# Modulation rows of a two-layer diffusion backbone: 128x2048 float32 pieces in four 32-column strips of the TensorE array, in place of 128x1024 pieces in 512-column blocks

## The chip, the cores and the metric

The kernel runs on one core of one Trainium2 chip. A core has five engines with instruction streams of their own: TensorE (PE, matrix products; its weight loads are shown apart as PEld), VectorE (DVE), ScalarE (ACT), GpSimd (POOL) and SyncE (SP, which only issues transfers here). They share an on-chip memory of 128 partitions (SBUF) and the accumulators that TensorE writes (PSUM); transfers to and from DRAM are moved by 16 DMA engines. Each engine works through its own instructions in order and waits on semaphores of the others.

The metric is the device time of one execution in microseconds (us). Before the change it is 3449.05 us, the median of three runs (3446.75 to 3449.51).

## The reference

Two layers work on 1024 latent tokens and 256 context tokens of width 1024. Layer 0 has neighbourhood attention beside a bidirectional mLSTM, layer 1 a bidirectional gated linear recurrence (HGRN2). What matters here is the modulation: each layer turns a conditioning vector into a shift, a scale and a gate of 1024 numbers each, once for the latent tokens (from `c`) and once for the context (from `c_ctx`).

```python
def _ada(cvec, w, b):
    m = jax.nn.silu(cvec) @ w + b
    return jnp.split(m.reshape((-1, 1, m.shape[-1])), 3, axis=-1)

for l in range(DEPTH):                       # DEPTH = 2, w_ada: (2, 1024, 3072) float32
    shift, scale, gate = _ada(c, w_ada[l], b_ada[l])
    shift_c, scale_c, gate_c = _ada(c_ctx, w_ada[l], b_ada[l])
    h_lat = _rms(x, norm_w[l]) * (1.0 + scale) + shift
    h_ctx = _rms(ctx, norm_w[l]) * (1.0 + scale_c) + shift_c
    ...                                      # the layer's mixer gives y_lat, y_ctx
    x = x + gate * y_lat
```

So two rows (`c` and `c_ctx`) are multiplied by a 1024x3072 matrix in each layer: 25 MB of weights in all for two rows of result. Columns 0 to 2047 of a layer are shift and scale, columns 2048 to 3071 the gate.

## The kernel before

**Precision and the main products.** Large products take each float32 operand as a sum of two parts in the faster type float32r, a high and a low one (`split`: a copy on ACT makes the high part, a subtraction on DVE the low part), and add three products (`dense`, lines 128 to 130: high by high, low by high or high by low). Their PSUM tiles are named `mm`.

**The first stage (the page's first 85 us).** The scope `pre` computes the modulation of layer 0 (`ada(0, pool, False)`), then normalizes ten tiles of 128 tokens (`x`; squares on ACT into `njk`, the inverse root `nr` on POOL, the scaling on DVE), transposes them on PE (line 238), applies scale and shift (`ntmp`) and splits the result into `hh` and `hl`, the input of every later projection. Meanwhile `na_values(0)` makes the first block of attention values on PE as far as `hh` and `hl` are there.

For layer 0, `ada_rows` loads the weights in pieces of 128x2x512 float32 (512 KB; two k-slices of 128 rows, 512 columns) through SP's queue. Each k-slice is one plain float32 product (line 179): the two conditioning rows stand in the array (128x2) and 512 columns of weights stream past. 4 blocks of 512 columns by 8 k-slices are 32 such products. A plain float32 product leaves two records in the trace, so they are 64 records. Each block ends with a copy on ACT (`adarow`, line 182) and four small products with the 2x2 identity `sel` (line 194) that turn the row into columns.

**The second stage (85 to about 250 us).** The scope `gates` computes the gates of the mLSTM (`ml_gates`), the gate rows of layer 0 (`ada_gate(0)`), shift and scale of layer 1 (`ada(1, pool, True)`), the gate rows of layer 1 (`ada_gate(1)`), and then `na_values(1)`, ten tiles of 128 tokens by 512 value columns (`proj_wide`). Here the modulation goes through the split: every piece of 512 KB comes through POOL's queue into one of three buffers (`adar`), ACT makes `adah` (128x1024), DVE makes `adal`, and PE does two float32r products for each k-slice and block (line 176 with four stationary columns, line 177 with two), 128 in all. A gate block ends with one product with `sel` (line 214) and a transfer to DRAM (`gated`), which is read only at the ends of the two layers.

**What sets the order.** A scheduler goes through the program in the order of the code, with a model of the chip, and puts each engine's instructions in a fixed order; `filler()` lowers the priority of the work in it, so that it is put where an engine would otherwise wait. What it has put in order, an engine does in that order. Tiles come from pools: a tile of a scope that opens can be written only when the tiles of the closed scope that lay in the same place are no longer read.

Of the kernel before, what the change touches and what calls it, by code (L numbers as in the profile page):

```python
# [44 lines left out]
class Prog:  # L45
# [114 lines left out]
    def ada_rows(self, l, blk, pool, parts):  # L160
        nc = self.nc
        wv = self.a["wada"][l].rearrange("(k p) f -> p k f", p=P)
        ps = self.ps("ad", [4, 512])
        for k in range(0, KD, 2):
            raw = self.t(pool, [P, 2, 512], F32, "adar", self.adab)
            self.last_dma = (nc.gpsimd if parts else nc.sync).dma_start(
                out=raw, in_=wv[:, k : k + 2, blk * 512 : (blk + 1) * 512]
            )
            if parts:
                hi = self.t(pool, [P, 2, 512], F32R, "adah", 2)  # L170
                lo = self.t(pool, [P, 2, 512], F32R, "adal", 2)
                self.split(hi, lo, raw)
            for j in range(2):
                first, last = k + j == 0, k + j == KD - 1
                if parts:
                    nc.tensor.matmul(ps, lhsT=self.sc4[:, k + j, :], rhs=hi[:, j, :], start=first, stop=False)
                    nc.tensor.matmul(ps[0:2], lhsT=self.sc4[:, k + j, 0:2], rhs=lo[:, j, :], start=False, stop=last)
                else:
                    nc.tensor.matmul(ps[0:2], lhsT=self.sc[:, k + j, :], rhs=raw[:, j, :], start=first, stop=last)
        rows = self.t(pool, [4, 512], F32, "adarow", 2)  # L180
        n = 4 if parts else 2
        nc.scalar.copy(rows[0:n], ps[0:n])
        return rows[0:n]

    def ada(self, l, pool, parts):
        nc, a = self.nc, self.a
        ab = self.ab[l]
        pss = self.t(pool, [P, 16, 2], F32, "adass", 1)
        for blk in range(4):
            rows = self.ada_rows(l, blk, pool, parts)  # L190
            p4 = self.ps("tr", [P, 4, 2])
            n = rows.shape[0]
            for m in range(4):
                nc.tensor.matmul(p4[:, m, :], lhsT=rows[:, m * P : (m + 1) * P], rhs=self.sel[0:n], start=True, stop=True)
            nc.vector.tensor_copy(pss[:, blk * 4 : blk * 4 + 4, :], p4)
        for v in range(2):

            nc.vector.tensor_tensor(out=ab[:, 1, v, :], in0=pss[:, 0:8, v], in1=self.badap[:, l, 0:8], op=ALU.add)
            nc.vector.tensor_tensor(out=ab[:, 0, v, :], in0=pss[:, 8:16, v], in1=self.badap[:, l, 8:16], op=ALU.add)
            nc.vector.scalar_tensor_tensor(  # L200
                out=ab[:, 0, v, :], in0=ab[:, 0, v, :], scalar=1.0, in1=self.normw[:, l, :], op0=ALU.add, op1=ALU.mult
            )

    def ada_gate(self, l, pool):
        nc, a = self.nc, self.a
        for blk in range(4, 6):
            s = slice((blk - 4) * 512, (blk - 3) * 512)
            gr = self.t(pool, [2, 512], F32, "grow", 1)
            bg = self.t(pool, [2, 512], F32, "bgrow", 1)
            for v in range(2):  # L210
                nc.sync.dma_start(out=bg[v : v + 1, :], in_=a["bada_g"][l : l + 1, s])
            rows = self.ada_rows(l, blk, pool, True)
            psg = self.ps("tr", [2, 512])
            nc.tensor.matmul(psg, lhsT=self.sel, rhs=rows, start=True, stop=True)
            nc.vector.tensor_tensor(out=gr, in0=psg, in1=bg, op=ALU.add)
            nc.sync.dma_start(out=self.gated[l, :, s], in_=gr)
# [50 lines left out]
    def na_values(self, b, pool=None):  # L267
        c0 = b * 256
        if pool:
            self.proj_wide(2 * D + c0, lambda s: self.vd[s, c0 : c0 + 512], pool, range(NT))  # L270
        else:
            self.proj_out(2 * D + c0, self.vd[:, c0 : c0 + 256])


    def proj_wide(self, c0, dst, pool, order, gate=None):
# [3 lines left out]
        for tt in order:  # L279
# [10 lines left out]
            nc.gpsimd.dma_start(out=d, in_=v)  # L290

# [71 lines left out]
    def ml_gates(self, pool, keep):  # L363
# [782 lines left out]
    def build(self):  # L1146
        tc, nc, a = self.tc, self.nc, self.a
        dma = nc.sync.dma_start
        with ExitStack() as es:
# [43 lines left out]
            self.sc4 = self.t(cp, [P, KD, 4], F32R, "sc4")  # L1193
            self.split(self.sc4[:, :, 0:2], self.sc4[:, :, 2:4], self.sc)
            self.sel = load("sel", [4, 2])
# [25 lines left out]
            with self.pp.phase(ad=2), tc.tile_pool(name="pre", bufs=2) as pool:  # L1221
# [390 lines left out]
```

## Time and profile before

| what | us |
|---|---|
| median of three runs | 3449.05 |
| the profiled execution | 3449.74 |
| its span, first to last instruction | 3448.0 |
| PE busy in the span | 3388.6 (98%) |
| DVE busy | 2089.0 (61%) |
| ACT busy | 1443.8 (42%) |
| POOL busy | 669.7 (19%) |

The profile is that of one execution. A row of a timeline reads: start, time until the last of the merged instructions ends, engine, line, operation, tiles written and read, shapes, count; in brackets how long the engine had been idle and what ended that. A matmul's duration includes its way through the array, so matmuls overlap in the records; how fast they follow one another is read from start to start. In a table of windows each engine's busy time stands beside the granted clock of TensorE (1.00 is full) and what the DMA engines moved.

### The profile page before, as it was taken

Reading aid. Unit: us, or ns where it says so; the run is one execution under the profiler, and the core shown is the slowest. Engines: PE = TensorE matmul, PEld = TensorE weight load, DVE = VectorE, ACT = ScalarE, POOL = GpSimd, SP = SyncE. Lnnn points to the kernel's source line nnn. Section 1 sums busy time; section 2 is a strip of 40 time slices with the busy share of each in tenths; the row PEclk is TensorE's granted clock in tenths of the full one; section 3 lists DMA queues with packets and bytes.
Section 4 is the critical chain, followed back from the end, with each engine's and each line's share of the span. In section 5 each row is a group of like instructions: output and inputs, shape, how many; then the busy total and the mean of one; then the engine's idle time right before and its main releaser. Section 6 shows DMA issues by size and latency. Waiting matters only on the chain.

```text
span 3448.0 us, 64658 instructions
## 1 busy us (share of the span) xinstructions
PE 3388.6 (98%) x25100; PEld 2988.2 (87%) x25100; DVE 2089.0 (61%) x4824; ACT 1443.8 (42%) x3353; POOL 669.7 (19%) x1044
## 2 busy tenths in 40 slices
PE   8999999999999999999999999999999999999987
PEld 5679998899989888898888999999999999989876
DVE  4536666666655556687656555555555555565667
ACT  5445544554443434454444333333333333333432
POOL 2222221222221112221100111111111111131023
PEclk9999999999999999999999999999999999999999
DMA  5542222322223434444653111111111111121374
GB/s 207 175 130 61 80 75 81 90 81 69 76 87 100 147 104 127 137 136 143 209 167 96 47 56 59 59 56 59 59 59 56 56 48 47 46 71 38 114 213 147
DMA packets 331539, 333.59 MB, mean 97 GB/s; under 512 B 30984, under 2 KB 277960, under 8 KB 331232
## 3 DMA queue, kind: packets, MB, share of 16 engines
q1 hardware_dynamic: 291008, 222.76, 21.9%
q0 software_dynamic: 40224, 106.69, 9.1%
q8 instruction: 198, 3.24, 0.4%
q14 instruction: 109, 0.89, 0.1%
HBM read 259.40 MB, written 69.79 MB: 95 GB/s over the span
## 4 chain that ended last, share of the span: by engine, by line
PE 91%; DVE 3%; DMA 2%; issue 1%; ACT 1%; POOL 0%; SPq 0%; POOLq 0%; DVEq 0%; ACTq 0%
PE mm L130 20%; PE mm L128 20%; PE mm L129 20%; PE s L1006 4%; PE acc L783 3%; PE tr L763 2%; PE mm L843 2%; PE mm L845 2%; PE mm L844 2%; PE acc L555 2%; PE s L564 2%; PE acc L545 1%; PE acc L1082 1%; PE acc L1083 1%; PE acc L1084 1%
## 5 line engine op out<-in xcount | busy, mean ns | idle before, releaser
L128 PE MATMUL mm<-hh,wh 128*128 128x512 f32 (+1 forms) x1600 | 582.2, 364 | 0.0
L130 PE MATMUL mm<-hh,wl 128*128 128x512 f32 (+1 forms) x1600 | 582.0, 364 | 0.0
L129 PE MATMUL mm<-hl,wh 128*128 128x512 f32 (+1 forms) x1600 | 581.7, 364 | 0.0
L128 PE MATMUL mm<-wh,hh 128*128 128x256 f32 (+1 forms) x1520 | 472.6, 311 | 1.3 <-ACT ev L317 0.6
L129 PE MATMUL mm<-wl,hh 128*128 128x256 f32 (+1 forms) x1520 | 471.6, 310 | 0.0
L130 PE MATMUL mm<-wh,hl 128*128 128x256 f32 (+1 forms) x1520 | 470.9, 310 | 0.0
L130 PEld LDWEIGHTS mm<-hh,wl 128*128 128x128 f32 x1600 | 301.9, 189 | 44.8 <-issue 0.2
L128 PEld LDWEIGHTS mm<-hh,wh 128*128 128x128 f32 x1600 | 302.1, 189 | 42.9 <-issue 0.5
L129 PEld LDWEIGHTS mm<-hl,wh 128*128 128x128 f32 x1600 | 302.0, 189 | 41.8 <-issue 0.2
L128 PEld LDWEIGHTS mm<-wh,hh 128*128 128x128 f32 x1520 | 290.0, 191 | 15.5 <-issue 1.1
L129 PEld LDWEIGHTS mm<-wl,hh 128*128 128x128 f32 x1520 | 289.9, 191 | 14.3 <-issue 2.9
L130 PEld LDWEIGHTS mm<-wh,hl 128*128 128x128 f32 x1520 | 289.9, 191 | 12.8 <-issue 1.7
L128 PE MATMUL mm<-wzh,hh 128*128 128x256 f32 x1024 | 293.8, 287 | 0.0
L130 PE MATMUL mm<-wzh,hl 128*128 128x256 f32 x1024 | 289.1, 282 | 0.0
L129 PE MATMUL mm<-wzl,hh 128*128 128x256 f32 x1024 | 288.6, 282 | 0.0
L73 DVE TENSOR_TENSOR wl<-wraw,wh 128x512 fp32r<-128x512 f32 x240 | 168.5, 708 | 119.4 <-ACT wh L72 113.0
L72 ACT CAST wh<-wraw 128x512 fp32r<-128x512 f32 x240 | 147.2, 619 | 211.9 <-PE mm L129 156.1
L128 PEld LDWEIGHTS mm<-wzh,hh 128*128 128x128 f32 x1024 | 192.9, 188 | 2.2
L129 PEld LDWEIGHTS mm<-wzl,hh 128*128 128x128 f32 x1024 | 192.8, 188 | 1.8
L130 PEld LDWEIGHTS mm<-wzh,hl 128*128 128x128 f32 x1024 | 192.7, 188 | 1.2
L843 PE MATMUL mm<-woh,yh 128*128 128x512 f32 x422 | 171.9, 407 | 14.8 <-ACT yh L72 8.3
L1036 ACT COPY gksel<-gK 128x1024 f32<-128x1024 f32 x96 | 111.0, 1156 | 178.1 <-PE s L1006 123.4
(391 smaller groups left out, 7518.2 us busy)
## 6 DMA issues: line engine op xcount, KB each, us to landing
wraw<-in_wab_dram SPq DMA_DIRECT2D x112, 256.0 KB
wraw<-in_wc_dram SPq DMA_DIRECT2D x96, 256.0 KB
wraw<-yd SPq DMA_DIRECT2D x94, 256.0 KB
adar<-in_wada_dram POOLq DMA_DIRECT2D x32, 512.0 KB, 4.4
wraw<-in_wc_dram SPq DMA_DIRECT2D x128, 128.0 KB
md<-ev POOLq DMA_DIRECT2D x60, 256.0 KB, 2.8
mloz<-md SPq DMA_DIRECT2D x40, 256.0 KB
adar<-in_wada_dram SPq DMA_DIRECT2D x16, 512.0 KB
```

Source lines behind the costliest of these rows:

```text
L72: nc.scalar.copy(hi, x)
L73: nc.vector.tensor_tensor(out=lo, in0=x, in1=hi.bitcast(F32), op=ALU.subtract)
L128: mm(ps, lhsT=lh(k), rhs=rh(k), start=(start and k == 0), stop=False)
L129: mm(ps, lhsT=lh(k), rhs=rl(k), start=False, stop=False)
L130: m = mm(ps, lhsT=ll(k), rhs=rh(k), start=False, stop=(stop and k == nk - 1))
L555: nc.tensor.matmul(num, lhsT=qc[:, j, :], rhs=C[d][:, j, :], start=False, stop=(j == 1))
L564: nc.tensor.matmul(u, lhsT=st["k"][c][:, j * P : (j + 1) * P], rhs=vw, start=True, stop=True)
L763: nc.tensor.transpose(pt[:nk, i, :], pr[:, o : o + nk], self.ident)
L783: m = nc.tensor.matmul(yp[h64], lhsT=v[:, h64], rhs=pTs[hd][:nk, i, :], start=(i == turn[0]), stop=(i == turn[-1]), tile_position=(0, hd * ...
L843: mm(ps, lhsT=yh[k], rhs=w.h(kk), start=(kk == 0), stop=False)
L1006: self.nc.tensor.matmul(out[s], lhsT=lhsT, rhs=rhs, start=True, stop=True, tile_position=(0, b * 64))
L1036: nc.scalar.copy(ksel.rearrange("p (b s i) -> p b s i", s=2, i=h), pick(K))
```

## The change

The change makes the modulation everywhere from the raw float32 weights, without the split.

- A piece of weights is now 128 rows by 2048 columns (1 MB). `ada_rows` returns eight steps for one output; a step loads a piece (`chunk`) and issues four plain float32 products, one for each 512 columns. The two conditioning rows are the first two of 32 stationary columns (`sc32`, the rest is zero, set in `wide_c`), and product j takes the strip of 32 columns of the array, and of 32 partitions of one PSUM tile, that begins at 32j (`tile_position`).
- Shift and scale of a layer are one output (2048 columns). The gates of both layers are another (1024 columns from each layer, so two transfers of 512 KB for a piece). There are 8 steps for layer 0, 8 for layer 1 and 8 for the gates, 32 products for each eight.
- An output of shift and scale ends with one copy on ACT (128x512), four small products with columns of the identity (line 194) and seven short operations on DVE. The gates end with one addition on DVE and four transfers.
- In the first stage the weights go first in SP's queue: no token tile may be loaded before the last piece of weights. `adar` has six buffers of 8 KB per partition, and the token tiles `x0` six buffers where there were ten.
- In the second stage the 16 steps of layer 1 and of the gates are handed to `ml_gates` (two after each of its three projections) and to `na_values(1)` (one after each value tile), with four buffers of 1 MB.

```diff
+    def ada_rows(self, srcs, pool, eng, done):
+        ps = self.ps("ad", [P, 512])
+        w = 2048 // len(srcs)
+
+        def chunk(k):
+            raw = self.t(pool, [P, 2048], F32, "adar", self.adab)
+            for i, src in enumerate(srcs):
+                self.last_dma = eng.dma_start(out=raw[:, i * w : (i + 1) * w], in_=src[k * P : (k + 1) * P])
+            for j in range(4):
+                self.nc.tensor.matmul(
+                    ps[32 * j : 32 * j + 32], lhsT=self.sc32[:, k, :], rhs=raw[:, j * 512 : (j + 1) * 512],
+                    start=(k == 0), stop=(k == KD - 1), tile_position=(0, 32 * j),
+                )
+            if k == KD - 1:
+                done(ps)
+
+        return [lambda k=k: chunk(k) for k in range(KD)]
...
+            for step in islice(steps, 1):
+                step()
...
             self.proj_tr(ps, w, 0, t0, n)
+            for step in islice(steps, 2):
+                step()
...
                 self.adab = 6
-                self.ada(0, pool, False)
+                self.wide_c(pool)
+                for step in self.ada(0, pool, nc.sync):
+                    step()
                 xts = {}
                 for tt in range(NT):
-                    xts[tt] = self.t(pool, [P, D], F32, "x0", NT)
-                    with tc.issue_after(self.last_dma.ins) if tt >= 2 else nullcontext():
+                    xts[tt] = self.t(pool, [P, D], F32, "x0", 6)
+                    with tc.issue_after(self.last_dma.ins):
                         dma(out=xts[tt], in_=self.xin(tt))
...
-                self.ml_gates(pool, mlk)
-                self.adab = 3
-                self.ada_gate(0, pool)
-                self.ada(1, pool, True)
-                self.ada_gate(1, pool)
-                self.na_values(1, pool)
+                self.adab = 4
+                self.wide_c(pool)
+                steps = iter(self.ada(1, pool, nc.gpsimd) + self.ada_gates(pool, nc.gpsimd))
+                self.ml_gates(pool, mlk, steps)
+                self.na_values(1, pool, steps)
```

SP's queue near the start of the program, before the change (`adar` are weights of the modulation, `x` token tiles, `wraw` weights of the first projection):

```order
L166 DMA adar_172<-in_wada_dram 128x2x512
L166 DMA adar_176<-in_wada_dram 128x2x512
L1228 DMA x_66_252<-in_x_dram 128x1024
L1228 DMA x_70_261<-in_x_dram 128x1024
L101 DMA wraw_604<-in_wab_dram 128x2x256
L101 DMA wraw_610<-in_wab_dram 128x2x256
L101 DMA wraw_616<-in_wab_dram 128x2x256
L166 DMA adar_180<-in_wada_dram 128x2x512
```

and after it:

```order
L173 DMA adar_174<-in_wada_dram 128x2048
L102 DMA wraw_559<-in_wab_dram 128x2x256
L102 DMA wraw_565<-in_wab_dram 128x2x256
L102 DMA wraw_571<-in_wab_dram 128x2x256
L173 DMA adar_180<-in_wada_dram 128x2048
L173 DMA adar_186<-in_wada_dram 128x2048
L1242 DMA x_48_207<-in_x_dram 128x1024
L1242 DMA x_52_216<-in_x_dram 128x1024
```

The two token tiles that were loaded after the first six half-size pieces now follow the eighth and last piece; six token tiles stand there one behind another, and the other four follow later in the queue, when a buffer is free.

PE in the second stage, in the second of the value tiles of `na_values(1)`, before the change:

```order
L130 MATMUL mm_1614<-wxh_1581,hl_132 128x512
L177 MATMUL ad_1186<-adal_1190,sc_29_108 2x512
L176 MATMUL ad_1186<-adah_1189,sc_29_108 4x512
L177 MATMUL ad_1186<-adal_1190,sc_29_108 2x512
L176 MATMUL ad_1186<-adah_1199,sc_29_108 4x512
L128 MATMUL mm_1642<-wh_1539,hh_131 128x512
L129 MATMUL mm_1642<-wl_1538,hh_131 128x512
```

and, in the first of them, after it:

```order
L129 MATMUL mm_1185<-wh_1162,hh_126 128x512
L130 MATMUL mm_1185<-wl_1161,hh_126 128x512
L175 MATMUL ad_869<-adar_1008,sc_173_866 32x512 x4
L131 MATMUL mm_1185<-wh_1162,hl_127 128x512
L129 MATMUL mm_1185<-wh_1168,hh_126 128x512
```

In place of float32r products that come one to four at a time between those of the projection, the four strip products of a piece (`x4`) stand together; PE then goes 14 to 24 products of the projection on to the next piece. The two pieces of a `ml_gates` step pair stand next to each other. In POOL's queue the first four pieces stand ahead of the last write of `na_values(0)`, and each later one between the writes of the value tiles. The last 250 us of the program are also put in a slightly different order (weight loads and splits of the output projection change places by a few rows), though no code of that stage is changed.

More of the change, by code (lines that the diff above doesn't have):

```diff
@@ L1 @@
[L1 removed]
+from contextlib import ExitStack, contextmanager
+from itertools import islice
 import numpy as np
@@ L156, in rsqrt @@
         g.tensor_tensor(out=out, in0=out, in1=self.mhalf[: out.shape[0], :n], op=ALU.pow)
[L160 to L183, printed above, removed]
@@ L186, in ada @@
+    def ada(self, l, pool, eng):
         nc, a = self.nc, self.a
         ab = self.ab[l]
[L188 to L192, printed above, removed]
-            for m in range(4):
-                nc.tensor.matmul(p4[:, m, :], lhsT=rows[:, m * P : (m + 1) * P], rhs=self.sel[0:n], start=True, stop=True)
-            nc.vector.tensor_copy(pss[:, blk * 4 : blk * 4 + 4, :], p4)
@@ L210, in ada_gate @@
             for v in range(2):
[L211 to L216, printed above, removed]
+                nc.sync.dma_start(out=bg[r + v : r + v + 1, :], in_=a["bada_g"][l : l + 1, b * 512 : (b + 1) * 512])
```

62 lines of the change are left out of this document (41 added, 21 removed).

## The prediction

> **What bounds the kernel now.** I read the page's chain of waits by engine first, and then the span cut into stages.
>
> ```profile
> span 3448.0 us, 64658 instructions
> ...
> PE 91%; DVE 3%; DMA 2%; issue 1%; ACT 1%; POOL 0%; SPq 0%; POOLq 0%; DVEq 0%; ACTq 0%
> ...
> core 0: us, PE busy (x) PEld busy (x) DVE busy (x) ACT busy (x) POOL busy (x), PEclk, DMA share, GB/s
> 0.00:28.00 28.00, 22.27 (x57) 5.46 (x58) 5.35 (x19) 7.38 (x14) 6.62 (x18) 1.00 0.96 330
> 0.00:40.00 40.00, 33.71 (x88) 8.20 (x88) 7.95 (x26) 10.78 (x21) 8.28 (x22) 1.00 0.98 351
> 28.00:44.00 16.00, 14.09 (x52) 4.99 (x50) 4.94 (x15) 7.32 (x14) 3.54 (x9) 1.00 1.02 395
> 40.00:85.00 45.00, 42.43 (x327) 41.20 (x328) 33.08 (x76) 34.64 (x82) 10.85 (x19) 0.92 0.22 74
> 85.00:91.00 6.00, 1.90 (x9) 0.75 (x8) 5.49 (x9) 2.67 (x3) 0.73 (x1) 0.86 0.83 296
> 91.00:250.00 159.00, 158.96 (x806) 119.12 (x807) 76.17 (x126) 69.75 (x110) 38.38 (x57) 0.98 0.52 157
> 250.00:3200.00 2950.00, 2933.55 (x22611) 2639.24 (x22609) 1795.00 (x4349) 1233.23 (x2958) 548.21 (x886) 1.00 0.28 84
> 3300.00:3400.00 100.00, 84.35 (x325) 65.24 (x324) 82.27 (x98) 37.77 (x67) 42.85 (x35) 0.90 0.74 226
> ```
>
> PE is the bound: 158.96 of 159 us busy from 91 to 250, 2933.55 of 2950 after that. So PE time taken out before 250 us moves everything behind it, and what ACT and DVE lose there (76.17 and 69.75 of 159 us busy) is worth nothing by itself. The first 40 us are different: the DMA engines are full (0.98). The change touches 0 to 250 us and, by the scheduler, the order of the tail.
>
> **The second stage: what goes.** The chain from 85 to 255 us by lines, and the removed splits in 85 to 250:
>
> ```profile
> by line: PE mm L130 24.6%; PE mm L128 24.4%; PE mm L129 24.4%; PE ad L177 8.8%; PE ad L176 8.7%; DMA adar<-in_wada_dram 2.9%; PE tr L194 2.3%; PE tr L214 2.2%; DVE wgl L73 0.7%; PE tr L420 0.6%; issue 0.6%; DVE wl L73 0.4%; PE tr L449 0.3%;
> ...
> L73 DVE TENSOR_TENSOR adal<-adar,adah 128x1024 fp32r<-128x1024 f32 x32 | 38.8, 1220 | 38.7 <-ACT adah L72 37.6 <-PE mm L129 1.0
> L72 ACT CAST adah<-adar 128x1024 fp32r<-128x1024 f32 x32 | 33.3, 1048 | 34.8 <-PE ad L176 33.4 <-DMA adar<-in_wada_dram 1.2
> ```
>
> Lines 176 and 177 hold 17.5% of 170 us, 29.7 us for 128 products (0.232 us each); line 194 holds 2.3%, 3.9 us for 16 small products; line 214 holds 2.2%, 3.7 us for 4. Sum off PE: 37.3 us. The 33.3 us of ACT and 38.8 us of DVE count zero: PE's products cover them today, and PE stays the cover.
>
> **What comes: 64 plain float32 products in strips.** Their price without overlap is in the first stage, and how strips overlap is in the attention stage, where two 64-column strips are used (line 783):
>
> ```profile
> 27.91 7.03 PE L179 MATMUL ad<-adar,cT 128*2 128x512 f32 x16
> 34.86 1.05 PE L194 MATMUL tr<-sel,adarow 2*128 2x2 f32 x8
> ...
> 315.37 0.27 PE L756 MATMUL acc<-ident,arb 128*128 128x128 f32 x1
> 315.57 0.33 PE L783 MATMUL acc<-apT,avw 72*64 72x128 f32 x2
> ...
> 315.84 0.61 PE L783 MATMUL acc<-apT,avc 128*64 128x128 f32 x8
> 316.27 0.61 PE L783 MATMUL acc<-apT,avw 96*64 96x128 f32 x8
> 316.81 0.75 PE L763 MATMUL tr<-ident,aP 128*96 128x128 f32 x5
> ```
>
> Sixteen records of line 179 take 34.86 - 27.91 = 6.95 us, 0.434 each; a product is two records (two passes), so 0.868 us. In strips, 8 records of 128 columns take 316.27 - 315.84 = 0.43 us, 0.054 each, while 0.434 us for 512 columns is 0.108 for 128: two strips run fully side by side. The window that holds just the first two records shows both done in 0.33 us, as long as one record lasts, so the first passes of both strips start together. I take the same for four strips: 0.868 us for a piece. The bounds are 0.868 and 4 x 0.868 = 3.47 us (no overlap); the row with strips is the nearest, so I stay at its end. Entering strips cost 315.57 - 315.37 - 0.108 = 0.09 us, leaving them 316.81 - 316.27 - 0.434 = 0.11: 0.2 us for a burst.
>
> The order has 16 pieces in 15 bursts, with one product of the first piece standing alone (one more 0.868): 17 x 0.868 + 15 x 0.2 = 17.8 us. Line 194 is now four products, a quarter of 3.9: 1.0 us. Added 18.8, removed 37.3: 18.5 us less PE time.
>
> The Trainium skill, TensorE: Matmul & The Clock Gate, Part 3, gives 2.38 times for three column strips instead of 3; at that efficiency a piece would take an estimated 1.09 us and the stage would be 3.8 us longer. The trace's two strips lose nothing, so the sum goes without it.
>
> **The start of the second stage.** DVE clears gate tiles and splits the gates' weights while PE waits:
>
> ```profile
> 81.92 0.27 DVE L437 MEMSET rtab<- 128x256 f32 x1
> ...
> 82.47 2.17 POOL L166 DMA_DIRECT2D adar<-in_wada_dram  x3 [1.07 <-DMA bgrow<-in_bada_g_dram]
> ...
> 86.72 1.04 ACT L72 CAST adah<-adar 128x1024 fp32r<-128x1024 f32 x1 [0.81 <-DMA adar<-in_wada_dram]
> ...
> 88.83 1.22 DVE wgl L73 x2
> ...
> 90.98 0.45 PE L449 MATMUL tr<-ident,rtab 128*128 128x128 f32 x1 [2.77 <-DVE gone L392]
> ```
>
> The transpose of the rope table (line 449) now stands behind 18 products of the gates, which need only the first `wgl` (89.4); against that DVE has two more short operations ahead (the clear and copy of `sc32`, of the size of the 0.27 us clear above), some 0.5 us. Bounds -1.1 and +0.5; I take -0.5 us.
>
> Transfers: half a piece took 86.72 - 82.47 = 4.25 us. A megabyte needs 0.524 MB / 395 GB/s = 1.3 us more, and POOL first clears `bgrow`: the first piece lands some 6 us after that place, the fourth about 8 us later, and longer where the projection's weights come in between. PE reaches them after the `wgl` wait and 18 products, some of them at half the clock, and the fourth after 26 more. So no wait here. Later PE needs 1 MB for every 24 products, 24 x 0.232 + 1.07 = 6.6 us or 159 GB/s, with three pieces ahead. The writes of the value tiles stand behind these loads in POOL's queue, each behind a load that waits for a piece consumed earlier than the tile it writes: no cost.
>
> **The first stage.** Today PE's products end it: 64 records at 0.434, and then the first token transposes.
>
> ```profile
> 5.29 13.17 PE L179 MATMUL ad<-adar,cT 128*2 128x512 f32 x24 [5.29 <-DMA adar<-in_wada_dram]
> ...
> 34.97 1.06 ACT L224 ACTIVATE njk<-x 128x1024 f32<-128x1024 f32 x1 [2.81 <-DMA x<-in_x_dram]
> ...
> 36.26 1.06 ACT L224 ACTIVATE njk<-x 128x1024 f32<-128x1024 f32 x1
> ...
> 38.53 0.75 DVE L226 TENSOR_SCALAR x<-x,nr 128x1024 f32<-128x1024 f32 x1 [0.71 <-POOL nr L156]
> ...
> 41.08 1.09 PE L238 MATMUL tr<-ident,x 128*128 128x128 f32 x8
> ...
> 80.71 1.10 DVE L262 TENSOR_TENSOR hl<-ntmp,hh 128x256 fp32r<-128x256 f32 x3 [0.23 <-ACT hh L261]
> ```
>
> After the change 8.39 MB of modulation weights and 0.79 MB of projection weights are ahead of the first token tile, 9.2 MB. Today 28 x 330 = 9.24 MB have come by 28 us, so the last piece lands at 28. A strip step (0.87) is shorter than its transfer (2.65 us at 395 GB/s), so the modulation is ready at about 31. The token tiles follow at 0.524 MB / 395 GB/s = 1.33 us: 29.3 and 30.7. From the square to the scaled tile it is 38.53 + 0.75 - 36.26 = 3.0 us, so both tiles of the first transposes are ready at 33.7 instead of 41.08: -7.4. What follows keeps its length: 41.08 to 85 us is PE's own work with a ramp in which tiles are normalized. Tiles 7 to 10 wait for a buffer, but PE comes to them one pair in some 9 us. The other bound is that two norms less are done by then (2 x 1.3 us) and PE, idle between pieces, starts with a lower clock, as it does today after its waits (0.92 and 0.86 granted in the two short stages above): -3. I take -6 us, near the bound that the transfers give.
>
> **The tail.** Rows change places in the last 250 us, where PE is idle 15.65 us in the hundred from 3300: between -4 and +4, taken as 0.
>
> **The sum.** 3449.74 (the profiled execution, 0.69 above the median) - 6 - 0.5 - 18.5 = 3424.7; less 0.7 for the median: **3424 us**.
>
> **Rivals.**
> *B, passes start strictly in their order.* A product's second pass then waits for its first in the same strip and holds back the next strip: only neighbouring passes overlap. A lone piece is 5 slots of 0.434 instead of 2; 64 products, 15 burst ends and the lone one make 80 slots: 34.7 + 3.0 + 1.0 = 38.7, 1.4 more than is removed; the first stage loses one end more, -4.7. 3449.74 - 4.7 - 0.5 + 1.4 - 0.7 = 3445. The joint start of the first two records above speaks against it; for four strips no row does. The same page and part of the Trainium skill says that matmuls start and end strictly in program order; by that rule this would be the result, and the trace has the joint start instead.
> *C, four strips run one after another (slower).* 64 x 0.868 + 3.0 + 1.0 = 59.6, 22.3 more than removed; in the first stage 8 x 3.47 us from the first landing near 6.6 (5.29, when half a piece is there, and 1.3) end at 34.3, and transposes start near 37 (-4): 3449.74 + 22.3 - 4 - 0.5 - 0.7 = 3467. It decides from a piece price p where 16p + 4 exceeds 37.3 + 6.5, p = 2.5 us; the line 783 rows speak against it.
> *D, the loads come late.* Were the second stage's 16.8 MB to come no faster than its 157 GB/s of today, they would take 107 us where PE needs some 90 (ten value tiles at 6.6 and the gates' 24): up to 17 us of waits and 3441. Against it, today's pace is set by the buffers (PE is never idle there), and 395 GB/s are shown.
>
> **How the numbers follow.** The forecast has 0.70 (its own range 3416 to 3432, by the bounds of the start and the tail and the price of four strips), B 0.13, C 0.07, D 0.07, anything else 0.03. To leave out no more than 2 in 10 the range must reach to B: 3416 to 3446. A measurement tells 0.2% (6.9 us) from no change: faster is the forecast, most of D and some of B, 0.82; same is the rest of B, 0.08; slower is C with a bad tail, 0.10.
>
> **What would show it.** Eight line 175 records of one piece within about 0.9 us from first to next operation (2.2 would be B, 3.5 C); the first token transposes near 34 us; no wait of PE on `adar` after the first pieces of the second stage; the tail as long as before. Wrong would be: pieces of 1.7 us or more, or idle PE ahead of line 175.

## The result: 4.5 us of the 25 that were forecast

The kernel before took 3447.76 us beside the changed one (median of 12 runs, 3441.56 to 3450.63), the changed kernel 3443.29 us (median of 12, 3439.72 to 3444.31). The ratio is 0.9987, with a 95% interval of 0.9978 to 0.9996: faster, by 4.5 us, where 25 were forecast. These 0.13% are less than the 0.2% that the prediction held to be measurable; with twelve runs of each the interval still stays clear of 1. The profiled execution of the changed kernel took 3444.31 us with a span of 3442.5; that of before had 3448.0, so the two profiles lie 5.5 us apart.

The same windows as in the prediction, of the changed kernel:

```profile
core 0: us, PE busy (x) PEld busy (x) DVE busy (x) ACT busy (x) POOL busy (x), PEclk, DMA share, GB/s
0.00:28.00 28.00, 11.40 (x56) 1.35 (x56) 4.13 (x17) 3.58 (x6) 4.58 (x13) 0.92 0.91 351
28.00:44.00 16.00, 12.37 (x64) 8.84 (x65) 10.56 (x26) 13.55 (x29) 5.85 (x13) 0.71 0.80 292
40.00:85.00 45.00, 40.89 (x306) 37.88 (x307) 34.83 (x77) 30.24 (x72) 10.69 (x18) 0.96 0.45 160
85.00:91.00 6.00, 6.00 (x25) 4.03 (x24) 0.73 (x5) 0.81 (x2) 0.00 (x0) 0.99 0.93 354
91.00:250.00 159.00, 158.04 (x913) 122.53 (x913) 55.21 (x117) 51.32 (x104) 34.19 (x54) 1.00 0.43 144
250.00:3200.00 2950.00, 2931.70 (x22530) 2628.93 (x22529) 1783.49 (x4318) 1219.57 (x2932) 547.45 (x882) 1.00 0.27 84
```

PE holds half as much in the first 28 us (11.40 against 22.27), is never idle from 85 to 91 us any more, and has 913 records from 91 to 250 us where it had 806. Behind that the picture looks the same as before, and that is where the gain goes.

The strips on PE's timeline:

```profile
18.39 1.07 PE L175 MATMUL ad<-adar,sc 128*32 128x512 f32 x8 [0.97 <-DMA adar<-in_wada_dram]
28.15 1.93 PE L175 MATMUL ad<-adar,sc 128*32 128x512 f32 x8 [0.58 <-DMA adar<-in_wada_dram]
...
32.88 0.45 PE L249 MATMUL tr<-ident,x 128*128 128x128 f32 x1
33.85 0.48 PE L249 MATMUL tr<-ident,x 128*128 128x128 f32 x1 [0.52 <-DVE x L237]
...
91.61 1.92 PE L175 MATMUL ad<-adar,sc 128*32 128x512 f32 x14
93.46 0.50 PE L131 MATMUL mm<-hh,wgl 128*128 128x512 f32 x1
```

A piece is 8 records (four strips, two passes each) within 1.07 us at full clock and 1.93 us at half clock; two pieces and their entry and exit take 93.46 - 91.61 = 1.85 us (two of the 16 records are missing from the trace). In the piece at 18.39 us the first passes of all four strips start within 0.02 us of one another, and the second passes 0.45 us later. The first token transposes start at 32.88 and 33.85 us in place of 41.08.

**Where the time went.** The same VectorE instructions were matched in the two traces and their starts compared (median at each place; minus is earlier than in the kernel before). This table holds all the runs told below; "tail" is the time from the landmark at 2900 us of the kernel before to the end. PE's products at the same places give the same figures to within 0.9 us. Each row is one execution, which lies up to 6 us from the median of its kernel (e12 and e4 the most), so differences of a few us between the ends of two rows are not to be relied on.

| kernel | at 250 us | at 1000 | at 2900 | end of the span | tail |
|---|---|---|---|---|---|
| before | 0 | 0 | 0 | 0 | 548.0 |
| changed | -25.1 | -22.6 | -11.6 | -5.5 | 554.1 |
| e1, 160 bytes put back | -26.8 | -28.9 | -20.2 | -14.3 | 553.9 |
| e2, 64 bytes | -25.0 | -25.1 | -7.1 | -1.8 | 553.3 |
| e3, 32 bytes | -25.2 | -25.3 | -13.7 | -7.3 | 554.4 |
| e4, before less 32 bytes | -1.0 | -0.3 | +13.2 | +15.9 | 550.4 |
| e5, 160 bytes on the right | -27.0 | -28.9 | -23.5 | -17.6 | 553.9 |
| e6, first stage alone | -9.4 | -8.5 | -6.1 | +0.9 | 555.0 |
| e7, second stage alone | -18.2 | -20.5 | -17.8 | -15.3 | 550.5 |
| e8, e1 with the tail's adds moved | -27.4 | -29.7 | -22.9 | -27.2 | 543.7 |
| e9, before with the tail's adds moved | -0.2 | -0.2 | +0.9 | -11.2 | 535.9 |
| e10, e1 with serial strips | +19.1 | +17.0 | +21.3 | +16.7 | 543.4 |
| e11, e1 with two x tiles early | -24.7 | -27.1 | -21.1 | -20.2 | 548.9 |
| e12, e8 with wz moved | -27.0 | -29.1 | -17.0 | -18.5 | 546.5 |
| e13, e1 with the old tail order | -25.5 | -27.6 | -23.4 | -25.2 | 546.2 |
| e14, its control | -23.2 | -25.4 | -21.2 | -15.3 | 553.9 |
| e15, all three | -26.4 | -28.7 | -22.7 | -34.6 | 536.1 |
| e16, old tail order alone | -25.3 | -22.6 | -9.1 | -12.0 | 545.1 |

The changed kernel is 25.1 us ahead at 250 us, as forecast. It loses 2.5 us of that up to 1000 us, 11.0 from there to 2900 us, and 6.1 behind 2900 us. None of this is work that the change touched.

Up to 2900 us the loss has no single wait behind it: the dense products themselves follow one another more slowly. From 950 us of the kernel before to 2900 us, and between the same two instructions of the changed kernel (first row before, second after):

```profile
950.00:2900.00 1950.00, 1939.18 (x14572) 1730.90 (x14571) 1180.81 (x2690) 778.66 (x1806) 333.08 (x593) 1.00 0.30 92
```

```profile
927.40:2888.40 1961.00, 1947.89 (x14569) 1733.42 (x14568) 1180.83 (x2683) 777.21 (x1801) 334.37 (x591) 1.00 0.30 92
```

The same products keep PE busy 8.7 us longer at the same granted clock of 1.00; the other 2.3 us are idle time of PE. All but some hundred of the 14570 records stand in the same order.

### The profile page after: what moved, and what is told of

The parts are those of the page before. It is cut to its first block, busy times and chain, and to the rows that moved or that the text cites. A ratio compares the mean times of both kernels' runs of the same rounds, so it can differ in the third digit from the quotient of the medians.

```text
span 3442.5 us, 64358 instructions
## 1 busy us (share of the span) xinstructions
PE 3368.1 (98%) x25044; PEld 2972.1 (86%) x25044; DVE 2051.4 (60%) x4786; ACT 1407.0 (41%) x3310; POOL 664.0 (19%) x1036
## 4 chain that ended last, share of the span: by engine, by line
PE 87%; DMA 4%; issue 3%; DVE 3%; ACT 1%; POOL 1%; SPq 0%; POOLq 0%; DVEq 0%; ACTq 0%
PE mm L129 19%; PE mm L131 19%; PE mm L130 19%; PE s L1021 4%; PE acc L798 2%; PE tr L778 2%; PE mm L858 2%; PE mm L859 2%; PE mm L860 2%; PE s L579 2%; PE acc L570 2%; PE acc L560 1%; PE acc L1097 1%; PE tr L1033 1%; PE acc L1098 1%
## 5 line engine op out<-in xcount | busy, mean ns | idle before, releaser
L129 PEld LDWEIGHTS mm<-wh,hh 128*128 128x128 f32 x1520 | 286.3, 188 | 22.7 <-ACT ev L295 4.2
L131 PEld LDWEIGHTS mm<-wh,hl 128*128 128x128 f32 x1520 | 286.2, 188 | 13.5 <-issue 1.4
L858 PE MATMUL mm<-woh,yh 128*128 128x512 f32 x422 | 169.8, 403 | 17.8 <-DVE og L1387 10.1
```

Source lines behind the costliest of these rows:

```text
L129: mm(ps, lhsT=lh(k), rhs=rh(k), start=(start and k == 0), stop=False)
L131: m = mm(ps, lhsT=ll(k), rhs=rh(k), start=False, stop=(stop and k == nk - 1))
L858: mm(ps, lhsT=yh[k], rhs=w.h(kk), start=(kk == 0), stop=False)
```

## The experiments

### The places of the tiles

Pools stack up from the low end of SBUF, those with `side="right"` from the high end. The constants lie lowest. The change drops `sc4` (128 bytes a partition) and `sel` (32 as allocated) from them, so in the built program every later tile of the left stack stands 160 bytes lower: the weights of all projections, all of attention and of both mixers. The inputs `hh` and `hl` stand on the right and did not move. Five kernels (e1 to e5) differ in nothing but such places; each engine's instructions and their order are those of the kernel that they start from.

**e1** puts the 160 bytes back, unused:

```diff
-            self.lb = self.t(cp, [P, 2, 16], F32, "lb")
+            cp.tile([P, 40], F32, tag="pad", name="pad"); self.lb = self.t(cp, [P, 2, 16], F32, "lb")
```

> The changed kernel with 160 unused bytes per partition put back in the constants' pool, where the two removed constant tiles stood; every instruction and its order are those of the changed kernel, and every tile of the left stack (weights of all projections, attention, gated and last mixer) stands at the address it had before the change. Placement theory (the shift by 160 bytes slows TensorE's products from 250 us on): the 14.5 us lost between 250 and 3000 us come back, ratio to the kernel before 0.9945, and up to 0.9925 if the 8 us lost behind 3000 us come back too; the 128x256 products of the last mixer at 0.1235, 0.1200 and 0.1190 us again. Rival, the pace is a matter of the chip or of the day, or follows from the changed order: ratio 0.9987 as the changed kernel, the products at 0.1258, 0.1219 and 0.1211 us.

Measured: 3432.02 us, ratio 0.9951 (0.9939 to 0.9964). By the two ratios 12.4 us come back. **e2** and **e3** put back 64 and 32 bytes (`[P, 16]` and `[P, 8]` in the same line).

> The changed kernel with 64 unused bytes per partition in the constants' pool: the tiles of the left stack move, but keep the remainder by 64 that the change gave them (32 bytes; 0 before). If the remainder by 64 sets the pace: 0.9987, as the changed kernel. If any other part of the address does (a bank of the memory, the distance to the tiles on the right side): different from the changed kernel, either way by up to 0.4%. If placement has no part in it: 0.9987.

> The changed kernel with 32 unused bytes per partition in the constants' pool: the large tiles of the left stack stand at multiples of 64 bytes again, but not at the addresses of before. If the remainder by 64 sets the pace: as with 160 bytes put back, 0.9945 (to 0.9925). If the exact address does: near 0.9987. If placement has no part in it: 0.9987.

Measured: 0.9994 (0.9985 to 1.0002) with 64 bytes, 0.9975 (0.9966 to 0.9984) with 32. So the place matters, but a multiple of 64 bytes is not the rule: with 32 bytes put back the large tiles stand at multiples of 64 again, and a third of the gain is there. **e4** goes the other way: the kernel before, with its left stack 32 bytes lower.

```diff
-            qkn = load("qkn", [P, 2])
+            qkn = self.t(cp, [P, 4], F32, "qkn"); nc.gpsimd.dma_start(out=qkn[:, 0:2], in_=a["qkn"])
 ...
-            self.sel = load("sel", [4, 2])
+            self.sel = qkn[0:4, 2:4]; nc.gpsimd.dma_start(out=self.sel, in_=a["sel"])
```

> The kernel before with the 4x2 selection rows kept in unused room of another constant, so that all tiles of the left stack stand 32 bytes lower, at a remainder of 32 by 64; every instruction stays. Placement theory: slower by the 14.5 us that the changed kernel lost between 250 and 3000 us, ratio 1.0042 (3462 us), and up to 1.0065 with the loss behind 3000 us. Rival, no part of placement: 1.0000 within 0.001.

Measured: 1.0035 (1.0023 to 1.0048), 12 us slower, with the old front and the old order. Which part of the address counts was then asked with **e5**: the left stack as the change has it, and the right stack lowered by the same 160 bytes.

```diff
-            nc.vector.memset(self.t(edge, [P, 8], F32, "edge"), 0.0)
+            nc.vector.memset(self.t(edge, [P, 48], F32, "edge")[:, 0:8], 0.0)
```

> The changed kernel with the 160 free bytes put under the right stack instead of the left: the inputs of the dense products (hh, hl) and the tiles of the output projections now stand 160 bytes lower too, so every distance between a left tile and a right tile is that of before, while no left tile stands at its address of before. Instructions and order are the changed kernel's. If the distance between the two operands of a product sets its pace: as with 160 bytes put back on the left, ratio 0.9951, the 128x256 products of the last mixer at 119 to 125 ns. If the left tile's own address does: as the changed kernel, 0.9987 (to 0.9994), 121 to 127 ns.

Measured: 0.9949 (0.9936 to 0.9961), as with the old addresses, though no tile of either stack stands where it stood. What counts is the distance between the two operands of a product. **e12** moves one group alone, on top of e8 (below): the weights `wz` of the last mixer (`wzh` is their high part), with the tiles of their pool behind them, 64 bytes up. 64 bytes of small tiles move to the constants for that, where 96 bytes of padding stand in place of 160.

```diff
-        w = self.wblock(pool, "wz", [col(3), col(4)], KD, 256)
+        pool.tile([P, 16], F32, tag="hpad", name=f"hpad{h}", bufs=1); w = self.wblock(pool, "wz", [col(3), col(4)], KD, 256)
 ...
-            ss = self.t(pool, [P, 4], F32, "gss", 2)
+            ss = self.t(self.cp, [P, 4], F32, "gss", 2)
```

> The run with the tail's adds moved, with the weights wz of the last mixer (and the tiles of that pool behind them) 64 bytes higher, so that wzh stands a whole multiple of 512 bytes below hh, as the weights w do; 64 bytes of small tiles move to the constants' pool. Everything else is the same, row for row. So far its distance to hh by 512 gave, for the 128x256 product hl after wzh: 64 bytes 119.0 ns, 96 bytes 122.2, 160 bytes 124.3, 192 bytes 121.8, 224 bytes 121.1. Theory (the best distance is a multiple of 512): under 118.5 ns, ratio 0.9910. Rival (64 bytes is a place as good as any, or the best): 119 to 124 ns, up to 12 us slower, ratio 0.9923 to 0.9955.

Measured: 0.9968 (0.9956 to 0.9979) against 0.9923 for e8: slower, as the rival has it and by a little more than it allowed, and the product took 123.9 ns. The weights `w` of the projections are at their best of the tried distances at a multiple of 512 (231.7 ns on average from one 512-column product to the next, 233.1 to 233.8 at the others), the weights `wz` at one of their worst. The two also stand the other way round in the array: there `hh` streams past `w`, here `wz` streams past `hh`. No run separates that from the distance. Below is the busy time of all products that read `wzh` between 1750 and 2890 us, 1728 of them, all at a granted clock of 1.00: in the kernel before, the changed kernel, e1, e5 and e12 (e8, from which e12 starts, has 331.35).

```profile
1750.00:2890.00 1140.00, 331.50 (x1728) 1.00 0.20 63
```

```profile
1750.00:2890.00 1140.00, 335.92 (x1728) 1.00 0.20 62
```

```profile
1750.00:2890.00 1140.00, 331.26 (x1728) 1.00 0.20 61
```

```profile
1750.00:2890.00 1140.00, 331.72 (x1728) 1.00 0.20 61
```

```profile
1750.00:2890.00 1140.00, 342.03 (x1728) 1.00 0.20 60
```

| distance of `wzh` to `hh`, by 512 bytes | 0 (e12) | 64 (before, e1, e5) | 96 (e4) | 160 (e2) | 192 (e3) | 224 (changed) |
|---|---|---|---|---|---|---|
| from product `hl` to the next, ns (mean) | 123.9 | 119.0 | 122.2 | 124.3 | 121.8 | 121.1 |

These means take in some longer steps; of the steps under 200 ns alone they are 119.9, 114.9, 118.1, 119.9, 117.6 and 116.8, in nearly the same order. That the distances repeat after 512 bytes is only how they are listed here, and not shown.

With the old distances PE is busy about as long as before again between the two instructions at 950 and 2900 us of the kernel before (1939.18 us there, 1947.89 in the changed kernel, 1942.71 in e1, 1940.71 in e5); in e13, told below:

```profile
922.40:2876.60 1954.20, 1939.96 (x14573) 1730.09 (x14572) 1179.95 (x2685) 776.70 (x1802) 334.80 (x591) 1.00 0.30 92
```

That the distance sets the pace is shown; by which rule is open. The Trainium skill, SBUF — State Buffer, section "SBUF: two separate sides", says that on the engines' side only the port pair that DVE and GpSimd share contends, and that PE never waits on anyone. Here 1728 products of unchanged size and order took between 331.3 and 342.0 us, depending on where one operand stood; the measurement decides, and what in the memory does it no run here shows.

### The parts of the change

**e6** is the kernel before with the new first stage alone, **e7** with the new second stage alone (the old functions kept beside the new ones, the constants' pool as large as before).

> The kernel before with the new first stage alone (four strips, x behind the weights), the second stage as before, all tiles that outlive these stages at their addresses of before. In the tail behind 3000 us the instructions stand almost as in the changed kernel (96 of 2166 TensorE rows moved, and 673 against the kernel before). Theory (the new order of the tail costs 9 us): the work is 6.0 us earlier at 250 us and this is lost behind 3000 us: ratio 1.0007 (0.9995 to 1.0020), with a TensorE wait of 7 us in the output projection for VectorE's og, as in the changed kernel. Rival, the tail's loss comes from elsewhere: 0.9982.

> The kernel before with the new second stage alone (layer 1 and gate rows in strips between the gate and value tiles), the first stage as before, addresses of before. The prediction gave this part 18.5 us and 0.5 us less start. Theory: 19 us earlier at 250 us; the tail has an order of its own (773 of 2182 TensorE rows moved against the kernel before), which costs between 0 and 9 us; with 3 to 6 us lost in the chunked mixer: ratio 0.9955 (0.9945 to 0.9985). Rival, the second stage gives less than the sum says: under 15 us earlier at 250 us.

Measured: e6 1.0006 (0.9997 to 1.0015), e7 0.9970 (0.9958 to 0.9981). By the table the first stage alone is 9.4 us ahead at 250 us (8.2 at 80 us, where it ends), more than the 6 forecast, and all of it is gone at the end: 3.3 up to 2900 us and 7.0 in the tail. The 7 us wait that was expected there stands in e6 too (7.0). The second stage alone is 18.2 ahead at 250 us, against 19.0 forecast; it keeps 15.3 in the profiled execution and 10.3 by the ratio.

**e10** gives the four strips of a piece four banks and the same columns of the array, so that they run one after another. Each strip then has a copy or an addition of its own at the end of an output.

```diff
-        ps = self.ps("ad", [P, 512])
+        ps = [self.ps("ad", [P, 512]) for _ in range(4)]
 ...
-                    ps[32 * j : 32 * j + 32], lhsT=self.sc32[:, k, :], rhs=raw[:, j * 512 : (j + 1) * 512],
-                    start=(k == 0), stop=(k == KD - 1), tile_position=(0, 32 * j),
+                    ps[j][0:32], lhsT=self.sc32[:, k, :], rhs=raw[:, j * 512 : (j + 1) * 512],
+                    start=(k == 0), stop=(k == KD - 1),
```

> The changed kernel with 160 bytes put back, where the four 32-column products of a weight piece go to four banks of PSUM at the same column strip, so that they cannot run side by side; pieces, queues and places in the program stay. Theory (the strips' overlap is what the second stage gains): a piece costs four times 0.868 in place of 0.868 us, 16 of them behind 87 us add 41.7 us; the first stage has as many 512-column products in a row as before and its transposes start near 41 us again, 7 later: ratio 1.009 (1.006 to 1.011), slower than the kernel before. Rival (the gain lies in the dropped split and its small matrices, the overlap is worth little): under 1.000.

Measured: 1.0050 (1.0037 to 1.0062), slower than the kernel before. On PE's timeline of e10, two pieces in the second stage:

```profile
107.34 7.05 PE L175 MATMUL ad<-adar,sc 128*32 128x512 f32 x16
```

3.5 us a piece against 0.93 in strips. At 250 us it is 45.9 us behind e1, close to the 48.7 that the terms give; the forecast of the ratio was too high because e10 loses less on the way and has a shorter tail (543.4 us). So the strips' overlap is what makes the second stage pay.

**e11** loads two tiles of x ahead of the first weights again, as before the change.

```diff
-                    with tc.issue_after(self.last_dma.ins):
+                    with tc.issue_after(self.last_dma.ins) if tt >= 2 else ExitStack():
```

> The changed kernel with 160 bytes put back and the first two tiles of x loaded ahead of the first modulation weights, as before the change. Theory (1 MB of x in front of 8 MB of weights on one path of some 350 GB/s): the weight pieces and with them the first transposes come 3 us later (36 to 37 us in place of 33), and the work at 250 us is 2 to 3 us later: ratio 0.9959 (0.9945 to 0.9970, the tail's order differing a little). Rival (the x tiles are only needed later, their queue place is free): first transposes near 33, ratio 0.9951.

```profile
35.11 2.17 PE L249 MATMUL tr<-ident,x 128*128 128x128 f32 x8
```

Measured: 0.9947 (0.9934 to 0.9959). The mechanism is there: the first transposes start at 35.11 us in place of 31.80 and 33.30 in e1, and at 250 us it is 2.1 us behind e1. But in the profiled executions the end comes 5.9 us earlier than in e1: this kernel's tail, in an order of its own, takes 548.9 us, 5.0 less, and e1 falls back by 3.0 us more between 250 and 2900 us. The ratio alone would have been read as "free".

### The tail

In the changed kernel's tail one wait of PE is twice as long as any before (7.0 us against 3.4). The waits of PE from 3200 us on (in all, times, longest), of the kernel before and then of the changed kernel:

```profile
PE mm L843 <- ACT yh L72: 6.3, 3, 3.4
PE mm L843 <- DVE og L1374: 6.2, 4, 2.6
PE mm L845 <- DVE yl L73: 2.4, 1, 2.4
PE s L1006 <- ACT gksel L1036: 2.2, 1, 2.2
PE mm L844 <- DVE wol L73: 1.3, 1, 1.3
```

```profile
PE mm L858 <- DVE og L1387: 10.1, 3, 7.0
PE mm L858 <- ACT yh L73: 5.8, 5, 1.9
PE mm L129 <- ACT yh L73: 3.9, 2, 3.5
PE mm L860 <- DVE yl L74: 2.2, 3, 1.6
PE s L1021 <- DVE gQ L1066: 0.9, 1, 0.9
```

What makes the 7.0 us stands on the timelines of DVE and POOL in the changed kernel:

```profile
3378.71 6.50 DVE L1438 TENSOR_TENSOR oys<-oyz,oys 128x512 f32<-128x512 f32 x2
3386.34 0.68 DVE L1387 TENSOR_TENSOR og<-mm,oe 128x512 f32<-128x512 f32 x1
```

```profile
3379.11 4.94 POOL L1387 TENSOR_TENSOR oacc<-os,oacc 128x512 f32<-128x512 f32 x4
```

Two DVE operations of 0.68 us each take 6.50, the first of them 5.90, while POOL does four adds in a row. The Trainium skill, SBUF — State Buffer, section "SBUF: two separate sides", calls the port pair an exclusive lock, and the loser blocks fully. The trace agrees: the DVE operation ends at 3384.61 us, behind the last of the adds (3384.05), and did not get in between them. On who gets the pair it is less clear, as by its record DVE began 0.40 us before the first add. So the first theory was that the new order puts these four adds where PE waits for DVE. **e8** takes e1 and gives the 28 adds that POOL does in the last projection to DVE; **e9** does the same to the kernel before, whose order on PE stays row for row.

```diff
-                    add(p[:, t, :], s6, p[:, t, :], nc.gpsimd)
-                    add(u[:, t, :], s6, u[:, t, :], nc.gpsimd)
+                    add(p[:, t, :], s6, p[:, t, :])
+                    add(u[:, t, :], s6, u[:, t, :])
 ...
```

> The changed kernel with 160 bytes put back, and the 28 adds of 128x512 that GpSimd does in the last output projection given to VectorE. With these adds on GpSimd, single VectorE two-input operations took 1.75 us in place of 0.68, and one 5.9 us beside four GpSimd adds in a row, 23.6 us over their usual time in all; 28 adds on VectorE are 19 us. Theory (the 7 us wait of TensorE in the tail is VectorE held up by GpSimd's four adds): that wait is gone, the tail is 5 to 9 us shorter, ratio 0.993 (0.992 to 0.9945). Rival, the wait comes from the order of the loads, or VectorE's own work takes its place: ratio 0.995 as with 160 bytes put back, with another wait of some 7 us.

> The kernel before with the same 28 adds of the last output projection given from GpSimd to VectorE as in the run with the tail's adds moved; TensorE's order stays that of before, row for row. Theory (the adds cost much only where the changed order puts four of them in a row in front of a VectorE operation that TensorE waits for): little to win here, 2 to 5 us, ratio 0.9990 (0.9980 to 1.0000). Rival (moving these adds is worth 10 us in any order, so that it says nothing on the change): 0.9970.

Measured: e8 0.9923 (0.9910 to 0.9937), 9.7 us less than e1 by the ratios, as expected. But e9 has 0.9976 (0.9966 to 0.9986): the same edit gives the kernel before 8.2 us. The theory falls. DVE behind POOL's adds is a cost of the tail in either order, and with it taken away the tails still lie 7.8 us apart (543.7 and 535.9).

What six kernels have in common is the order itself: the changed kernel, e1, e2, e3, e5 and e6 have the same order behind 2900 us (e6 nearly) and take 553.3 to 555.0 us there; before, e4 and e10, with the other order (e10 nearly), take 543.4 to 550.4. The order is thus not all: these three differ by 7.0 us among themselves. The scheduler settles the tail from its own model of when things end, and a shift far ahead tips it one way or the other. **e13** and **e14** use that: 12 and 40 transposes that nobody reads, at the end of the second stage of e1. With 12, all but some 120 of the 3800 records of PE in the tail stand in the order of the kernel before; with 40, all in that of the changed kernel.

```diff
                 self.na_values(1, pool, steps)
+                for _ in range(12):
+                    nc.tensor.transpose(self.ps("tr", [P, P]), self.ident, self.ident)
```

> The changed kernel with 160 bytes put back and 12 idle 128x128 transposes of the identity at the end of the second stage (some 0.11 us each, 1.3 us in all; nobody reads them). They shift the scheduler's model so that behind 3000 us every queue has the order of the kernel before again (31 of 2182 TensorE rows moved, none on the other engines). Theory (the order of the tail alone costs some 6 us): 548 us from the landmark at 2900 us to the end in place of 553.9, ratio 0.9938 (0.9925 to 0.9950). Rival (the tail is longer for another reason that the front brings along): 554 us there, ratio 0.9955.

> The same with 40 idle transposes (4.4 us), with which the scheduler puts the tail in the changed kernel's order again (607 of 2182 TensorE rows moved against the kernel before). Theory (the order of the tail alone costs some 6 us): 554 us from the landmark to the end, ratio 0.9964. Rival (idle transposes in front, or a later start, shorten the tail by themselves): 548 us there, ratio 0.9947.

Measured: e13 3423.53 us, 0.9924 (0.9911 to 0.9938); e14 3431.38 us, 0.9953 (0.9941 to 0.9965). From the landmark to the end, e13 and then e14:

```profile
2876.60:3422.80 546.20, 514.59 (x3811) 448.83 (x3809) 335.47 (x507) 188.53 (x379) 118.86 (x142) 0.97 0.33 103
```

```profile
2878.80:3432.70 553.90, 516.37 (x3811) 449.56 (x3810) 334.51 (x507) 187.84 (x379) 119.12 (x142) 0.96 0.32 101
```

7.7 us between two kernels that differ in 28 idle transposes; those cost 2.3 us at 250 us. 5.9 of the 7.7 are idle time of PE. In e13's tail the longest wait on `og` is 2.6 us, as before, in e14's 6.9, as in the changed kernel. The order is shown to be the cause; which of its changed places costs what was not separated.

**e16** restores the order alone, in the changed kernel; **e15** joins e13 with the adds of e8.

> The changed kernel with the 12 idle transposes alone: the tail's order of before, the tiles' places of the changed kernel. Theory: some 4.6 us less than the changed kernel (5.9 less 1.3), ratio 0.9974 (0.9960 to 0.9985), since what the tiles' places cost is lost ahead of the tail. Rival: 0.9990 or more.

> The changed kernel with 160 bytes put back, the tail's order of before through 12 idle transposes, and the tail's 28 adds on VectorE. If the three repairs add up: from the run with the tail's adds moved (0.9923) by 536 in place of 543.7 us in the tail and 1.3 us of transposes, ratio 0.9905 (0.989 to 0.992), 3415 us. Rival (the two tail repairs take away the same waits): 0.9923 or more.

Measured: e16 3437.14 us, 0.9965 (0.9953 to 0.9978); e15 3416.05 us, 0.9906 (0.9893 to 0.9920), where 0.9905 was worked out from the single repairs: they add up. From e16 to e13, which differ in the 160 bytes alone and ran on one chip, it is 13.6 us. e15 is the fastest kernel of this case: 32.5 us under the kernel before and some 28 under the changed one.

## Why the prediction was wrong

**The strips: right.** Four strips run side by side: 0.93 us a piece where 0.868 and 0.1 for half a burst were forecast, and 3.5 without overlap (e10). So rivals B and C are refuted; C as built in e10, with the tiles in place, took 3466.5 us, where the rival was priced at 3467; that they meet so closely is luck, as e10 loses 4.3 us between 1000 and 2900 us and has a tail 4.6 shorter than before. The 2.38 of the Trainium skill for three strips (TensorE: Matmul & The Clock Gate, Part 3) would make a piece an estimated 1.09 us, slower than these four are; the trace has 3.5 / 0.93 = 3.8 for four.

**The second stage: right.** 18.5 us of PE time and 0.5 of its start were forecast. The changed kernel gains 25.1 - 7.3 = 17.8 us from 80 to 250 us, and e7 18.2: about 1 us less than forecast. PE waits for `adar` 0.3 us once, so rival D is refuted too.

**The first stage: right.** The last piece was forecast to land at 28 us; it is multiplied at 28.15. The transposes start at 32.88 and 33.85 where 33.7 was forecast. The term took 6 us of the 7.4 that the transfers gave, for fear of a lower clock. The clock is lower, 0.71 from 28 to 44 us where it was 1.00, and still the same VectorE instructions at 80 us come 7.3 us earlier (8.2 in e6). Both stages make 25.1 us; the forecast was 25.0. That the sum is met to 0.1 us is luck: the first stage gave 1.3 us more than its term, the second 1.2 less.

**The step that failed** stands at the head of the argument: "So PE time taken out before 250 us moves everything behind it." It does, if what stands behind keeps its duration, and that was taken for granted: the sum has no term for 250 to 2900 us, where 13.5 us were lost (25.1 ahead at the one place, 11.6 at the other). The list of what the change removes left out where `sc4` and `sel` lay. Their 160 bytes moved every tile of the left stack, and that costs 13.6 us (e13 against e16; 12.4 by e1 and the changed kernel; a shift of 32 bytes costs the kernel before 12.1, e4). None of the rivals had a cost between 250 us and the tail; it fell under "anything else", which had a chance of 0.03.

**The tail: the second mis-sized term.** It was taken as 0 between -4 and +4 and is +6: 554.1 us where 548.0 were. e13 and e14 show that the order does it.

With both undone, e13 takes 3423.53 us; the forecast was 3424. To meet it so closely is luck in part: e13 holds 1.3 us of idle transposes, still loses 4.2 us between 1000 and 2900 us, and its tail is 1.8 us shorter than before.

**What stays open.** Between 1000 and 2900 us, e1, e5, e13 and e14, with the old distances, still lose 4.2 to 8.7 us; the kernel before with moved adds (e9) loses 1.1 there and e10 4.3. In e1, from 950 us of the kernel before on, 5.2 us are more idle time of PE, in single waits of up to 1.1 us on DVE, ACT and one transfer, and 3.5 more busy time. These are single executions, and the five runs of e1 spread over 10.7 us. No run asked why.

## What to carry to other kernels

Dropping a small constant is not free of consequences when it lies at the bottom of a stack: compare the places of the large operands, and the start-to-start times of untouched products, before a lost gain is put down to waits. Where a scheduler fixes the order from a model, any change in front reshuffles what comes last; read the order there, and try a harmless shift of the model to see what another order gives, since a gain of a few us can be hidden or faked by it (e6, e11). Follow a gain by landmarks: the start of the same instructions in both traces, every few hundred us, shows at which place it is lost, which the end alone does not.

## What the runs showed of the hardware that was not expected

- The distance between the two operands of a float32r product sets its pace at full clock: 119.0 to 124.3 ns for 256 columns against `wzh`, 231.7 to 233.8 ns for 512 columns against `w` (means). At one distance (a multiple of 512 bytes) the one is near its worst and the other best.
- A DVE operation with two inputs in SBUF that meets adds on GpSimd takes 1.75 to 1.79 us in many cases of the tail (3377.00 us in the changed kernel) in place of 0.68, and 5.90 beside four adds in a row. Moving 28 adds to DVE saves 8 to 10 us (e8, e9).
- The clock falls after short waits in the tail. In the kernel before, in windows of 5 us behind a wait of 2.15 us that ends at 3236.08, and then in the changed kernel around the 7.0 us wait that ends at 3387.07:

```profile
3235.00:3240.00 5.00, 3.33 (x35) 2.49 (x36) 5.00 (x9) 3.20 (x6) 0.00 (x0) 0.64 0.99 311
3240.00:3245.00 5.00, 5.00 (x16) 3.93 (x16) 5.00 (x8) 4.78 (x10) 0.00 (x0) 0.68 1.08 336
```

```profile
3380.00:3385.00 5.00, 0.12 (x1) 0.00 (x0) 5.00 (x2) 1.07 (x2) 4.05 (x4) 0.74 0.26 94
3385.00:3390.00 5.00, 2.93 (x7) 2.35 (x8) 5.00 (x10) 0.00 (x0) 0.00 (x0) 0.50 0.23 83
3390.00:3395.00 5.00, 5.00 (x17) 3.96 (x17) 5.00 (x9) 2.76 (x5) 2.83 (x2) 0.73 0.64 211
3395.00:3400.00 5.00, 5.00 (x23) 3.99 (x23) 5.00 (x7) 1.39 (x3) 2.68 (x3) 1.00 0.76 271
```

Behind the 7.0 us wait full clock is back some 6 us after PE goes on (half from 3385 to 3390, 0.73 in the next window), so this wait costs an estimated 3 us more than its length.
